# Paired last experts, earlier transposes, and split work moved from GpSimd to VectorE in a two-block transformer kernel

## The chip, the cores and the metric

One core of a Trainium2 chip runs the whole program. TensorE multiplies matrices, VectorE and ScalarE work on tiles and read TensorE's results out of PSUM, GpSimd does some work on tiles too, SyncE issues the loads of weights. Each engine runs its own queue in program order and waits on semaphores for the others. The metric is the time of one launch in device microseconds (us), lower is better.

## The reference, cut to what matters

256 tokens of width 1024 go through two blocks. The first block (an SGU with differential attention, memory attention, then a layer of 32 experts, two per token) is followed by a norm and by the second block: a layer with a convolution and a layer with causal attention, each between two SwiGLU FFNs of inner width 2816.

```python
def swiglu(x, w_gate, w_up, w_down):
    return (jax.nn.silu(x @ w_gate) * (x @ w_up)) @ w_down
...
def expert_rows(args):
    xb, e = args
    g = xb @ w_gate[e]
    u = xb @ w_up[e]
    return (jax.nn.silu(g) * u) @ w_down[e]
...
# layer 1 of the second block: 12 heads of 64, one block of keys, causal
s_own = jnp.einsum('bhqd,bhjd->bhqj', q_c, k_own).astype(jnp.float32) * scale
s_own = jnp.where(k_pos[None, :] <= q_pos[:, None], s_own, -jnp.inf)
...
h = h + jnp.concatenate([primary, mem_out], axis=-1) @ w_o[layer]
h = h + 0.5 * swiglu(rms_norm_2(h, ffn2_norm_g[layer]), ...)
```

## The kernel before, in words

**Products in three passes.** In the second block an fp32 product is made of three fp32r ones: hi by hi, lo by hi, hi by lo. `split` makes hi (a copy on ScalarE, L174) and lo (raw minus hi, L175) of each tile of weights, 2048 columns in four pieces of 512 or in two of 1024. lo runs on VectorE unless a caller gives `lo_engine`; `values` and the attention's output projection give GpSimd. `xT` transposes the tokens X and `hilo` splits them: on ScalarE (L201) and VectorE (L202) for the inputs, which the traces call x, x.

**The experts.** `Moe.run` takes the experts in eight groups of E = 4, each with C = 32 slots, so that four experts share one 128-row tile. `weights` streams gate, up and down (two raw tiles of 1 MB per expert and matrix; the last group's in halves of 512 KB), `some` multiplies: gate, up, `hidden` (silu by up), `hidden_T` (four transposes, L866, and a copy, L868), down. All four experts of a group go through each of these steps together.

**The FFNs.** `Ffn.run` works on 11 chunks of 256 inner columns; a chunk's weights are two `half` tiles (h0, h1) of 512 input rows each. `ahead` splits chunk 0's two halves early. The first chunk is multiplied as the tokens are transposed: the tokens come in pieces of two (`xT(..., range(2))`, then `range(2, 4)` as `more`). The second chunk uses `ws[0]` and `ws[1]`; then `turned` transposes g, the hidden of chunk 0 (L1053), splits it into hh and hl, and `down` multiplies it by w_down into acc.

**The causal attention.** `Second.attention` makes queries (`heads`: norm, rope, transposes at L1463), then values in three steps (`values`), with `head_pair` steps between: scores, two mask products per head (a 128x128 mask times the identity, for the diagonal blocks of the two token tiles), softmax (maximum L340, exponential L345, reciprocal L346, scaling L1238), transposes, product with the values. Then `out_proj` multiplies by w_o in four chunks c0 to c3.

**What sets the order.** The code's generators are stepped by hand (`step`, `drain`), and the tile framework's scheduler orders each engine's queue by that and by what is ready; `issue_after(ins)` keeps an instruction behind ins in that order. The second block has three raw buffers and three of hi and of lo; a load waits for the splits that read its buffer.

Of the kernel before, what the change touches and what calls it, by code (L numbers as in the profile page):

```python
# [10 lines left out]
F32 = mybir.dt.float32  # L11
# [6 lines left out]
P = 128  # L18
# [653 lines left out]
class Moe:  # L672
# [180 lines left out]
    def hidden(self, w2, gb, ub):  # L853

        k, nc = self.k, self.k.nc
        h = w2.tile([P, 512], F32, tag="mh", name=k.name("mh"), bufs=1)
        nc.scalar.activation(h, gb, AF.Silu)
        nc.vector.tensor_tensor(out=h, in0=h, in1=ub, op=ALU.mult)  # L858
        return h

    def hidden_T(self, w2, h, tag="mm"):
        k, nc = self.k, self.k.nc
        hb = k.bank(tag)
        h = h.rearrange("s (p i) -> s i p", i=4)
        for f in range(4):
            nc.tensor.transpose(hb[:, f * P : (f + 1) * P], h[:, f, :], k.ident)  # L866
        hT = w2.tile([P, 4, P], F32, tag="mhT", name=k.name("mhT"), bufs=1)
        nc.scalar.activation(hT, hb.rearrange("p (f s) -> p f s", f=4), AF.Copy)  # L868
        return hT
# [25 lines left out]
    def weights(self):  # L895


        k, a = self.k, self.k.a
        for e in range(0, 32, E):
            for nm, i in (("w_gate", 8), ("w_up", 8), ("w_down", 4)):  # L900
                for half in range(2):
                    w = [k.raw() for _ in range(E)]
                    n = 2 if e >= 32 - E else 1
                    for c in range(n):
                        c = slice(2048 * c // n, 2048 * (c + 1) // n)
                        for j in range(E):
                            src = a[nm][0, e + j].rearrange("(p i) n -> p (i n)", i=i)[:, 2048 * half : 2048 * half + 2048]
                            k.nc.sync.dma_start(w[j][:, c], src[:, c])
                    yield [v.rearrange("p (a b) -> p a b", a=i // 2) for v in w]

    def some(self, w2, xg, side, pending, ws):

        k = self.k
        slots = [slice(j * C, (j + 1) * C) for j in range(E)]
        banks = []
        for _ in range(2):
            b = k.bank()
            for half in range(2):
                w = next(ws)
                for i in range(4):  # L920
                    kk = 4 * half + i
                    for j, s in enumerate(slots):
                        k.mm(b[s, :], xg[half][:, i, s], w[j][:, i, :], kk == 0, kk == 7)
# [769 lines left out]
```

## Time and profile before

| what | value |
|---|---|
| median of 3 runs | 1687.4 us (1686.13 to 1688.68) |
| profiled execution's own time | 1684.22 us |
| its span | 1682.6 us, mean granted clock 0.984 |
| TensorE busy | 1564.2 us, 93% |
| VectorE, ScalarE, GpSimd busy | 790.7 us, 676.0 us, 102.5 us |
| loads from HBM | 406.70 MB |

The span runs from the first to the last instruction; the execution's own time is 1.6 us more, and the median is 3.2 us above that. The stages, as the timeline has them: first block without experts to about 260 us, experts to about 701, FFN to 890, convolution layer to 995, two FFNs to 1390 (the keys among them), causal attention to 1495, last FFN to the end.

### The profile page before, as it was taken

The page shows a single profiled execution, that of the slowest core. Times are in us where ns is not written, and L with a number is a line of the kernel's source. Part 1 is how long each engine was busy: PE and PEld are TensorE (multiplying, and loading weights), DVE is VectorE, ACT ScalarE, POOL GpSimd, SP SyncE. Part 2 cuts the span into 40 slices and gives each one's busy share as a digit, 9 for nine tenths or more (in the row PEclk, how much of TensorE's full clock was granted, in tenths as well). Part 3 has the DMA queues.
Part 4 walks back from the last instruction along what each step waited for, and adds up shares of the span by engine and source line. Part 5 has one row for each costly group of instructions (what it writes and reads, how often), then busy time and mean ns, then how long its engine had stood idle before and what let it go on. Part 6 is the DMA issues. An engine that isn't in the chain of part 4 may idle for free.

```text
span 1682.6 us, 21321 instructions
## 1 busy us (share of the span) xinstructions
PE 1564.2 (93%) x8326; PEld 1118.4 (66%) x8326; DVE 790.7 (47%) x1478; ACT 676.0 (40%) x1265; POOL 102.5 (6%) x122
## 2 busy tenths in 40 slices
PE   8999998868868878899999999999999999999999
PEld 7888873312212222388889878888788887688887
DVE  5875661101011101365556875555665456655544
ACT  7556641000000000254446464444654446654442
POOL 3100000000000000002000010000010004410000
PEclk9999999999999999999999999999999999999999
DMA  8638479999999999955655636565555553345552
GB/s 281 200 131 298 162 273 390 420 421 421 420 421 421 421 420 410 368 164 176 218 185 178 190 104 198 176 200 176 174 196 180 182 193 126 101 150 186 190 187 88
DMA packets 182997, 412.10 MB, mean 245 GB/s; under 512 B 10618, under 2 KB 127564, under 8 KB 161388
## 3 DMA queue, kind: packets, MB, share of 16 engines
q1 hardware_dynamic: 180630, 409.81, 67.7%
q8 instruction: 67, 1.10, 0.3%
q10 hardware_dynamic: 2086, 0.72, 0.2%
q14 instruction: 38, 0.31, 0.1%
q0 software_dynamic: 176, 0.17, 0.0%
HBM read 406.70 MB, written 1.05 MB: 242 GB/s over the span
## 4 chain that ended last, share of the span: by engine, by line
PE 55%; DMA 25%; DVE 2%; ACT 1%; issue 1%; POOL 0%; SPq 0%; ACTq 0%; POOLq 0%; DVEq 0%
PE mm L80 35%; PE acc L80 18%; DMA raw<-in_w_down_dram 8%; DMA raw<-in_w_up_dram 8%; DMA raw<-in_w_gate_dram 8%; PE mm L1053 1%; PE mm L213 1%; DVE lo L175 1%; DMA raw<-in_ffn_w_up_dram 1%; ACT hi L174 0%; PE mm L1223 0%; DVE ne L1238 0%; POOL hst L90 0%; SPq L1016 0%; DVE rope L1443 0%
## 5 line engine op out<-in xcount | busy, mean ns | idle before, releaser
L175 DVE TENSOR_TENSOR lo<-raw,hi 128x512 fp32r<-128x512 f32 (+1 forms) x596 | 468.1, 828 | 294.4 <-ACT hi L174 293.2
L80 PE MATMUL mm<-hi,x 128*128 128x512 f32 (+1 forms) x1728 | 549.3, 391 | 4.6 <-DVE x L202 3.6
L174 ACT ACTIVATE hi<-raw 128x512 fp32r<-128x512 f32 (+1 forms) x620 | 415.2, 724 | 339.0 <-PE mm L80 141.4
L80 PEld LDWEIGHTS mm<-hi,x 128*128 128x128 f32 x1728 | 324.4, 189 | 70.0 <-DVE x L202 4.1
L80 PE MATMUL mm<-lo,x 128*128 128x512 f32 (+1 forms) x864 | 334.7, 387 | 1.7 <-DVE lo L175 1.7
L80 PE MATMUL mm<-raw,xg 128*32 128x512 f32 x1024 | 200.8, 676 | 75.6 <-DMA raw<-in_w_up_dram 43.6
L80 PEld LDWEIGHTS mm<-raw,xg 128*32 128x32 f32 x1024 | 42.8, 121 | 224.0 <-DMA raw<-in_w_up_dram 87.9
L80 PEld LDWEIGHTS mm<-lo,x 128*128 128x128 f32 x864 | 163.6, 189 | 33.2 <-DVE lo L175 2.4
L80 PE MATMUL acc<-hi,hh 128*128 128x512 f32 x352 | 138.1, 392 | 0.0
L80 PE MATMUL acc<-lo,hh 128*128 128x512 f32 x352 | 137.1, 389 | 0.0
L80 PE MATMUL acc<-hi,hl 128*128 128x512 f32 x352 | 136.6, 390 | 0.0
L858 DVE TENSOR_TENSOR mh<-mh,mm 128x512 f32<-128x512 f32 x8 | 5.5, 687 | 257.7 <-PE mm L80 257.7
L80 PE MATMUL mm<-x,hi 128*128 128x256 f32 x640 | 118.7, 286 | 2.1 <-DVE x L202 1.1
L80 PE MATMUL acc<-hi,x 128*128 128x512 f32 (+1 forms) x352 | 110.2, 386 | 2.0 <-ACT x L198 2.0
L80 PE MATMUL acc<-raw,mhT 128*32 128x512 f32 x512 | 104.6, 598 | 5.9 <-DMA raw<-in_w_down_dram 5.0
L80 PEld LDWEIGHTS mm<-x,hi 128*128 128x128 f32 x640 | 100.0, 191 | 4.3 <-DVE x L202 1.8
L80 PE MATMUL mm<-x,lo 128*128 128x256 f32 x320 | 90.5, 283 | 0.0
L1043 ACT ACTIVATE g<-mm,rs 128x256 f32<-128x256 f32 x88 | 41.5, 475 | 112.0 <-PE mm L80 110.6
L80 PEld LDWEIGHTS acc<-hi,x 128*128 128x128 f32 x352 | 65.2, 188 | 15.9 <-ACT x L198 2.9
L80 PEld LDWEIGHTS acc<-hi,hh 128*128 128x128 f32 x352 | 66.1, 188 | 14.5 <-ACT hh L198 1.5
L80 PEld LDWEIGHTS acc<-hi,hl 128*128 128x128 f32 x352 | 66.1, 188 | 14.4 <-DVE hl L199 0.5
L80 PEld LDWEIGHTS acc<-lo,hh 128*128 128x128 f32 x352 | 66.1, 188 | 13.4
(346 smaller groups left out, 1326.0 us busy)
## 6 DMA issues: line engine op xcount, KB each, us to landing
raw<-in_w_gate_dram SPq DMA_DIRECT2D x56, 1024.0 KB
raw<-in_w_up_dram SPq DMA_DIRECT2D x56, 1024.0 KB
raw<-in_w_down_dram SPq DMA_DIRECT2D x56, 1024.0 KB
raw<-in_ffn_w_gate_dram SPq DMA_DIRECT2D x88, 512.0 KB
raw<-in_ffn_w_up_dram SPq DMA_DIRECT2D x88, 512.0 KB
raw<-in_ffn_w_down_dram SPq DMA_DIRECT2D x44, 1024.0 KB
raw<-in_w_in_dram SPq DMA_DIRECT2D x9, 1024.0 KB
raw<-in_w_kv_mem_dram SPq DMA_DIRECT2D x8, 1024.0 KB
```

The source lines that it names most:

```text
L80: return self.nc.tensor.matmul(out, l, r, start=start, stop=stop, skip_group_check=True).ins
L174: nc.scalar.activation(hi[:, c], v[:, c], AF.Copy)
L175: ins = lo_engine.tensor_tensor(out=lo[:, c], in0=v[:, c], in1=hi.bitcast(F32)[:, c], op=ALU.subtract).ins
L213: nc.tensor.transpose(b[:, kk * S + t * P : kk * S + (t + 1) * P], X[:, t, k * P : (k + 1) * P], self.ident)
L858: nc.vector.tensor_tensor(out=h, in0=h, in1=ub, op=ALU.mult)
L1043: nc.scalar.activation(g, b[:, :S], AF.Silu, scale=rs[:, t : t + 1])
L1053: nc.tensor.transpose(b[:, j * S + t * P : j * S + (t + 1) * P], gs[t][:, j * P : (j + 1) * P], k.ident)
```

## The change

Six edits. (1) In the last group of experts (28 to 31) gate is loaded and multiplied for all four, up, hidden, transposes and down in two pairs. (2) Before the first FFN of the second block, the split of chunk 0's second half comes behind the first pieces of x, with both loads issued as before. (3) In every FFN the last k of four of `ws[1]` is multiplied after `turned`. (4) The second part of the values' weights and w_o of the attention get their lo on VectorE. (5) A head's two mask products become one, with a mask kept twice. (6) The first step of the output projection, its splits too, is ordered behind the copy of the values.

```diff
-    def hidden(self, w2, gb, ub):
+    def hidden(self, w2, gb, ub, h=None, r=slice(0, P)):
...
+        gb, ub = k.bank(), k.bank()
+        wide(gb, range(E))
+        h, hTs = None, []
+        for n, js in enumerate(parts):
+            r = slice(js[0] * C, (js[-1] + 1) * C)
+            wide(ub, js)
+            h = self.hidden(w2, gb, ub, h, r)
+            if n == len(parts) - 1 and pending is not None:
+                pending()
+            hTs.append(self.hidden_T(w2, h, "mm", r, ("mhT", "oh")[n]))
...
+                    each = [(hf, v, j) for hf in range(2) for v, j in zip(w, js)]
+                    if last and f == 3:
+                        each.sort(key=lambda t: t[2])
...
     def ahead(self):
-        self.pre = [self.half(0, h, 4) for h in range(2)]
+        for _ in self.ahead_by_half():
+            pass
+
+    def ahead_by_half(self):
+        v = [self.loaded(0, h) for h in range(2)]
+        self.pre = []
+        for h in range(2):
+            self.pre.append(self.k.split(v[h], pieces=4))
+            yield
...
         gs = hidden(b0)
-        k.proj_tok(b1, ws[1], x, 4, 4, False, True)
+        k.proj_tok(b1, tuple(v[:, :3] for v in ws[1]), x, 4, 3, False, False)
         h = turned(gs)
+        k.proj_tok(b1, tuple(v[:, 3:] for v in ws[1]), x, 7, 1, False, True)
...
-            k.proj_tok(banks, k.wrows(a["w_kv_2"], 512 * kk, 1024, 512, nc.gpsimd), x, 4 * kk, 4, kk == 0, kk == 1)
+            k.proj_tok(banks, k.wrows(a["w_kv_2"], 512 * kk, 1024, 512), x, 4 * kk, 4, kk == 0, kk == 1)
...
-            nc.scalar.activation(self.v[:, t, 256:], banks[t][0], AF.Copy, scale=rs[:, t : t + 1])
+            self.v_ins = nc.scalar.activation(self.v[:, t, 256:], banks[t][0], AF.Copy, scale=rs[:, t : t + 1]).ins
...
-            k.mm(sc[j][:, :P], self.identr, self.maskr, False, True)
-            k.mm(sc[j][:, 2 * P : 3 * P], self.identr, self.maskr, False, True)
+            k.mm(sc[j].rearrange("p (a b) -> p a b", a=2)[:, :, :P], self.identr, self.maskr, False, True)
...
-        out = k.out_proj(w_o, cat, ahead=ahead, lo_engine=nc.gpsimd)
-        step(out, att, out, att)
+        out = k.out_proj(w_o, cat, ahead=ahead)
+        with k.tc.issue_after(self.v_ins):
+            step(out)
+        step(att, out, att)
...
-                F[1, 0].ahead()
+                pre = F[1, 0].ahead_by_half()
+                step(pre)
...
                 k.xT(X, [(x, fg)], range(2))
+                with tc.issue_after(k.behind[1]):
+                    step(pre)
```

VectorE's queue where the first FFN of the second block begins: lo are the low parts of the weights (first h0, then h1, then chunk 1), x the low parts of the tokens. Before:

```order
L175 TENSOR_TENSOR lo_4761<-raw_4757,hi_4760 128x512 x4
L175 TENSOR_TENSOR lo_4774<-raw_4770,hi_4773 128x512 x4
L202 SCALAR_TENSOR_TENSOR x_4756<-mm_4793,fg,x_4755 128x256
L202 SCALAR_TENSOR_TENSOR x_4756<-mm_4802,fg,x_4755 128x256
L1249 TENSOR_REDUCE cmask<-ident 128x32
L202 SCALAR_TENSOR_TENSOR x_4756<-mm_4793,fg,x_4755 128x256
L202 SCALAR_TENSOR_TENSOR x_4756<-mm_4802,fg,x_4755 128x256
L1275 MEMSET ch 128x6x2
```

After:

```order
L175 TENSOR_TENSOR lo_4773<-raw_4766,hi_4772 128x512 x4
L202 SCALAR_TENSOR_TENSOR x_4765<-mm_4792,fg,x_4764 128x256
L202 SCALAR_TENSOR_TENSOR x_4765<-mm_4801,fg,x_4764 128x256
L1282 TENSOR_REDUCE cmask<-ident 128x32
L1308 MEMSET ch 128x6x2
L202 SCALAR_TENSOR_TENSOR x_4765<-mm_4792,fg,x_4764 128x256
L202 SCALAR_TENSOR_TENSOR x_4765<-mm_4801,fg,x_4764 128x256
L175 TENSOR_TENSOR lo_4811<-raw_4769,hi_4810 128x512 x4
```

The first two x, in the order before behind eight lo, stand behind four, and h1's four lo behind all four x of the first pieces.

TensorE's queue in the same FFN, at the end of the second chunk (mm<-hi,x and mm<-lo,x its products, mm<-ident,g the transposes of chunk 0's hidden, acc the down product). Before:

```order
L80 MATMUL mm_4892<-hi_4909,x_4755 128x512
L80 MATMUL mm_4892<-lo_4910,x_4755 128x512
L80 MATMUL mm_4892<-hi_4909,x_4756 128x512
L1053 MATMUL mm_4996<-ident,g_4966 128x128 x2
L1053 MATMUL mm_4996<-ident,g_4969 128x128 x2
L80 MATMUL mm_5047<-hi_5052,x_4755 128x512
L80 MATMUL mm_5047<-lo_5053,x_4755 128x512
L80 MATMUL mm_5047<-hi_5052,x_4756 128x512
L80 MATMUL mm_5047<-hi_5052,x_4755 128x512
L80 MATMUL acc_4819<-hi_5013,hh_5001 128x512
```

After:

```order
L80 MATMUL mm_4901<-lo_4919,x_4764 128x512
L80 MATMUL mm_4901<-hi_4918,x_4765 128x512
L1085 MATMUL mm_4999<-ident,g_4975 128x128 x2
L1085 MATMUL mm_4999<-ident,g_4978 128x128 x2
L80 MATMUL mm_4900<-hi_4918,x_4764 128x512
L80 MATMUL mm_4900<-lo_4919,x_4764 128x512
L80 MATMUL mm_4900<-hi_4918,x_4765 128x512
L80 MATMUL mm_4901<-hi_4918,x_4764 128x512
L80 MATMUL mm_4901<-lo_4919,x_4764 128x512
L80 MATMUL mm_4901<-hi_4918,x_4765 128x512
L80 MATMUL acc_4828<-hi_5022,hh_5004 128x512
```

The transposes stand six products earlier, ahead of the last k, and acc's first product directly behind that k.

VectorE's queue in the softmaxes of the causal attention, at the third pair of heads (smx the maxima and reciprocals, ne the scaled weights, x a split of the attention's output). Before:

```order
L340 TENSOR_REDUCE smx_10931<-acc_10921 128x1
L346 RECIPROCAL smx_10931<-smx_10931 128x1
L340 TENSOR_REDUCE smx_10937<-acc_10921 128x1
L1238 TENSOR_SCALAR ne_10933<-ne_10933,smx_10931 128x128
L340 TENSOR_REDUCE smx_10943<-acc_10922 128x1
L199 TENSOR_TENSOR x_10672<-mm_10955,x_10671 128x256
L346 RECIPROCAL smx_10937<-smx_10937 128x1
L1238 TENSOR_SCALAR ne_10939<-ne_10939,smx_10937 128x256
L346 RECIPROCAL smx_10943<-smx_10943 128x1
L340 TENSOR_REDUCE smx_10949<-acc_10922 128x1
L1238 TENSOR_SCALAR ne_10945<-ne_10945,smx_10943 128x128
```

After:

```order
L340 TENSOR_REDUCE smx_10935<-acc_10927 128x1
L175 TENSOR_TENSOR lo_11245<-raw_11242,hi_11244 128x512
L346 RECIPROCAL smx_10935<-smx_10935 128x1
L340 TENSOR_REDUCE smx_10941<-acc_10927 128x1
L1271 TENSOR_SCALAR ne_10937<-ne_10937,smx_10935 128x128
L340 TENSOR_REDUCE smx_10947<-acc_10928 128x1
L199 TENSOR_TENSOR x_10682<-mm_10959,x_10681 128x256
L175 TENSOR_TENSOR lo_11245<-raw_11242,hi_11244 128x512
L346 RECIPROCAL smx_10941<-smx_10941 128x1
L346 RECIPROCAL smx_10947<-smx_10947 128x1
L340 TENSOR_REDUCE smx_10953<-acc_10928 128x1
L1271 TENSOR_SCALAR ne_10943<-ne_10943,smx_10941 128x256
```

Two of the four lo of w_o's first chunk, which stood in GpSimd's queue, stand here between the steps of the softmaxes; the other two follow, and c1 and c2 are spread over the next pairs in the same way, twelve in all.

## Rows read from the trace of the kernel before

**Rows 1.** Page, part 1: busy us, share of the span, instructions.

```profile
PE 1564.2 (93%) x8326; PEld 1118.4 (66%) x8326; DVE 790.7 (47%) x1478; ACT 676.0 (40%) x1265; POOL 102.5 (6%) x122
```

**Rows 2.** Chain that ended last, 640 to 720 us: start, length, what.

```profile
705.68 4.82 DVE lo L175 x8
710.50 0.41 DVE x L202
...
710.95 3.78 PE mm L80 x8
714.74 1.46 PE mm L213 x8
```

**Rows 3.** Timeline of TensorE, 672 to 712 us: start, length, [idle before].

```profile
682.15 0.75 PE L866 MATMUL mm<-ident,mh 128*128 128x128 f32 x4 [0.85 <-DVE mh L858]
683.64 18.15 PE L80 MATMUL acc<-raw,mhT 128*32 128x512 f32 x64 [0.75 <-ACT mhT L868]
...
710.95 1.65 PE L80 MATMUL mm<-hi,x 128*128 128x512 f32 x3 [3.65 <-DVE x L202]
```

**Rows 4.** Timeline of TensorE's weight loads, 683 to 702 us.

```profile
699.89 0.14 PEld L80 LDWEIGHTS acc<-raw,mhT 128*32 128x32 f32 x2 [0.30 <-DMA raw<-in_w_down_dram]
```

**Rows 5.** Windows: length, busy (instructions) by engine, granted clock, DMA.

```profile
704.00:708.00 4.00, 2.87 (x14) 1.54 (x12) 4.00 (x7) 4.00 (x9) 0.00 (x0) 1.00 0.69 195
710.00:712.00 2.00, 1.05 (x3) 0.85 (x4) 2.00 (x6) 1.01 (x3) 0.00 (x0) 0.50 1.08 353
716.00:718.00 2.00, 2.00 (x11) 1.64 (x10) 1.79 (x4) 1.35 (x4) 0.00 (x0) 1.00 0.19 70
```

**Rows 6.** Chain that ended last, 720 to 760 us.

```profile
719.88 15.42 PE mm L80 x68
735.31 0.44 PE mm L1053 x4
...
736.67 5.65 PE acc L80 x24
...
752.75 5.44 PE acc L80 x24
```

**Rows 7.** Timeline of ScalarE, 724 to 733 us.

```profile
729.87 0.84 ACT L1043 ACTIVATE g<-mm,rs 128x256 f32<-128x256 f32 x2 [0.75 <-DVE rs L1591]
```

**Rows 8.** Timeline of VectorE, 1409 to 1422 us.

```profile
1411.00 1.77 DVE L1125 TENSOR_TENSOR bk<-bk,hst 128x512 f32<-128x512 f32 x1 [1.25 <-POOL hst L90]
1412.69 1.77 DVE L175 TENSOR_TENSOR lo<-raw,hi 128x512 fp32r<-128x512 f32 x1
1414.39 2.62 DVE L1443 TENSOR_TENSOR rope<-bk,rope_tab 128x128 f32<-128x128 f32 x2
```

**Rows 9.** Timeline of GpSimd, 1406 to 1470 us.

```profile
1410.93 5.93 POOL L175 TENSOR_TENSOR lo<-raw,hi 128x512 fp32r<-128x512 f32 x4
```

**Rows 10.** Chain that ended last, 1380 to 1500 us.

```profile
1407.11 0.69 DVE bk L1125
...
1418.66 7.24 PE mm L80 x48
1425.90 1.45 PE acc L80 x12
```

**Rows 11.** Timeline of TensorE, 1415 to 1420 us.

```profile
1418.03 0.63 PE L1463 MATMUL mm<-ident,bk 128*128 128x128 f32 x4 [3.32 <-DVE bk L1445]
```

**Rows 12.** Windows in the attention, columns as in group 5.

```profile
1420.00:1422.00 2.00, 2.00 (x12) 2.00 (x11) 1.58 (x7) 1.67 (x4) 0.17 (x1) 0.50 0.85 332
1440.00:1470.00 30.00, 26.75 (x182) 17.19 (x181) 22.45 (x84) 23.22 (x79) 7.36 (x6) 1.00 0.29 94
1444.00:1448.00 4.00, 2.42 (x20) 1.59 (x20) 3.50 (x10) 3.13 (x12) 3.37 (x3) 1.00 0.76 251
```

**Rows 13.** Timeline of VectorE, 1438 to 1456 us.

```profile
1444.87 1.37 DVE L1238 TENSOR_SCALAR ne<-ne,smx 128x128 f32<-128x128 f32 x1
...
1450.10 0.27 DVE L1238 TENSOR_SCALAR ne<-ne,smx 128x128 f32<-128x128 f32 x1
```

More of the change, by code (lines that the diff above doesn't have):

```diff
@@ L898, in weights, with parts, some, wide @@
         k, a = self.k, self.k.a
+        every = range(E)
         for e in range(0, 32, E):
+            last = e + E == 32
+            parts = self.parts(last)
+            n = 2 if last else 1
             for nm, i in (("w_gate", 8), ("w_up", 8), ("w_down", 4)):
[L901 to L911, printed above, removed]
+                for js in (every,) if nm == "w_gate" else parts:
+                    for half in range(2):
+                        w = [k.raw() for _ in js]
+                        for c in range(n):
+                            c = slice(2048 * c // n, 2048 * (c + 1) // n)
+                            for v, j in zip(w, js):
+                                src = a[nm][0, e + j].rearrange("(p i) n -> p (i n)", i=i)[:, 2048 * half : 2048 * half + 2048]
+                                k.nc.sync.dma_start(v[:, c], src[:, c])
+                        yield [v.rearrange("p (a b) -> p a b", a=i // 2) for v in w]
+    def parts(self, last):
+        return (range(E // 2), range(E // 2, E)) if last else (range(E),)
+    def some(self, w2, xg, side, pending, ws, last):
         k = self.k
+        parts = self.parts(last)
         slots = [slice(j * C, (j + 1) * C) for j in range(E)]
-        banks = []
-        for _ in range(2):
-            b = k.bank()
+        def wide(b, js):
             for half in range(2):
@@ L921, in some @@
                     kk = 4 * half + i
-                    for j, s in enumerate(slots):
-                        k.mm(b[s, :], xg[half][:, i, s], w[j][:, i, :], kk == 0, kk == 7)
-            banks.append(b)
-        h = self.hidden(w2, *banks)
-        if pending is not None:
-            pending()
-        hT = self.hidden_T(w2, h)
-        y = [k.bank("acc") for _ in range(2)]
-        for half in range(2):
-            w = next(ws)
-            for i in range(2):
-                f = 2 * half + i
-                for hf in range(2):
-                    for j, s in enumerate(slots):
-                        k.mm(y[hf][s, :], hT[:, f, s], w[j][:, i, hf * 512 : hf * 512 + 512], f == 0, f == 3)
+                    for v, j in zip(w, js):
+                        k.mm(b[slots[j], :], xg[half][:, i, slots[j]], v[:, i, :], kk == 0, kk == 7)
+        gb, ub = k.bank(), k.bank()
[8 more added lines that the diff above has]
+            hTs.append(self.hidden_T(w2, h, "mm", r, ("mhT", "oh")[n]))
+        y = [k.bank("acc") for _ in range(2)]
+        for n, js in enumerate(parts):
+            for half in range(2):
+                w = next(ws)
+                for i in range(2):
+                    f = 2 * half + i
+                    each = [(hf, v, j) for hf in range(2) for v, j in zip(w, js)]
+                    if last and f == 3:
+                        each.sort(key=lambda t: t[2])
+                    for hf, v, j in each:
+                        l = hTs[n][:, f, slots[j - js[0]]]
+                        k.mm(y[hf][slots[j], :], l, v[:, i, hf * 512 : hf * 512 + 512], f == 0, f == 3)
         return self.combine(w2, y, *side)
@@ L994, in run @@
                 side = self.scatter_side(w2, oh, self.W[:, :, e : e + E])
-                pending = self.some(w2, xg, side, pending, weights)
+                pending = self.some(w2, xg, side, pending, weights, e + E == 32)
                 with tc.issue_after(ready):
@@ L1010, in half, with loaded @@
     def half(self, c, h, pieces=2):
+        return self.k.split(self.loaded(c, h), pieces=pieces)
+    def loaded(self, c, h):
         k = self.k
```

23 lines of the change are left out of this document (13 added, 10 removed).

## Prediction

> **What bounds the kernel now.** I read the busy shares first: TensorE has 1564.2 of 1682.6 us [rows 1]. Every other engine is at half of that or below, so a saving counts only where TensorE, or the loads during the experts, stand still for it. The chain that ended last then shows where TensorE stood still at the places that the change touches, the timelines say for what, and windows show the granted clock there. Three places matter.
>
> At the first FFN of the second block the chain goes through eight lo on VectorE (705.68, 4.82 us), one x, and then eight products [rows 2]. TensorE waited 3.65 us for that x [rows 3]. The granted clock was 1.00 (2.4 GHz) from 704 to 708, while TensorE was busy for 2.87 of 4 us; it fell to 0.50 (1.2 GHz) during this wait and was 1.00 again from 716 [rows 5]. So the eight products took 3.78 and the eight transposes behind them 1.46 us.
>
> In the attention TensorE waited 3.32 us for a bk, a key or query after rope [rows 11]. Ahead of that stand a bk and a lo of 1.77 us each and two rope operations of 2.62 [rows 8], where another bk of the same shape took 0.69 [rows 10]. At that time GpSimd ran four lo, 5.93 us from 1410.93 on [rows 9]. After the wait the granted clock was 0.50 once more from 1420 to 1422 [rows 12], and 48 products took 7.24 us [rows 10].
>
> From 1440 to 1470, in the softmaxes, no engine is full: TensorE 26.75, VectorE 22.45, ScalarE 23.22 of 30 us [rows 12]. They take turns, so here the length hangs on VectorE and ScalarE.
>
> **The change part by part.** All terms are against the profiled execution, 1684.22 us.
>
> *Experts in pairs.* The last group's loads keep their sizes and their number, and the last load is followed by the same four passes. What a pair can save is TensorE's wait for hidden, 0.85 and 0.75 us [rows 3]. But TensorE is still waiting for a load of w_down at 699.89 [rows 4], after the 64 down passes began at 683.64: both waits are made up long before the end, and the loads set it. Silu, product and copy run twice on half the partitions; the first pair's lie under the second pair's loads, and the second pair's cost what the four's did. I take 0. If the waits were not covered, it could give up to 1.6 back or cost as much again; I keep -0.3 to +0.3, since only the order of the last passes differs.
>
> *The first FFN's split behind x.* Four lo of the eight go behind the x: four of 4.82/8 = 0.60 us, 2.4 us. TensorE would resume at 708.5, after 1.2 us of waiting instead of 3.65. With so short a wait I take the clock to stay at 1.00. At that level a product takes 15.42/68 = 0.227 us [rows 6], eight 1.81, and eight transposes 2 x 0.44 = 0.88 [rows 6]. Instead of 3.78 + 1.46 = 5.24 us that is 2.69: another 2.5 us. The four lo that now come later follow the four x and end at about 712.7. TensorE has the eight products, the eight transposes (to 711.2) and twelve more products of h0, 2.7 us, ahead of the first one of h1, at 713.9: covered by 1.2 us, and each lo of h1 serves a later product than the one ahead of it. Without the cover TensorE would wait up to 1 us. Later loads that wait for h1's buffer go out 2.2 us later and are not next. Together -4.9, bounds -2.4 (the clock falls all the same) and -5.2.
>
> *Transposes earlier.* Directly after the transposes of g, the 24 products of acc take 5.65 us, elsewhere 5.44 [rows 6]; they wait for hh and hl. Six products more between, 1.4 us, cover that. It happens in four FFNs: 4 x 0.21 = -0.8. The opposite danger is that g is late. The first two g start at 729.87 on ScalarE [rows 7], the transposes at 735.31 [rows 6]. The transposes come 1.4 us earlier, and in this first FFN all of TensorE's queue another 4.9, so here they stand at about 729. The g wait for a norm factor [rows 7], which comes from X by way of ScalarE and VectorE; I take it to be 2 to 3 us earlier, since both stood waiting for x before, and g then to be ready at about 728.6. If it were not earlier, TensorE would wait some 2 us there. I take -0.8, bounds +1.0 and -1.0.
>
> *GpSimd's lo to VectorE, up to the values.* Without the four lo beside them, bk goes back from 1.77 to 0.69 us, lo from 1.77 to 0.60, and the two rope operations, at the same ratio, from 2.62 to about 1.0: 3.8 us, more than the wait of 3.32, so the wait goes: -3.3. With no wait the clock should stay up; 48 products of 256 columns at half of 0.227 are 5.5 us instead of 7.24: -1.7. VectorE gets eight lo of the values, 4.8 us, of which the 3.8 us freed pay most.
>
> *One mask per head.* 12 score and mask products take 1.45 us [rows 10], 0.12 each, which is what a product of 256 columns takes too (5.5/48 = 0.115). So two for four saves 0.24 a pair of heads. For the first two pairs this is on TensorE's path: -0.5. The other four lie in the softmax section, where TensorE has room: 0. The Trainium skill, in "TensorE: Matmul & The Clock Gate", section "Back-to-back issue gap", speaks against this term: the time between two products grows with the columns, so one of 256 costs as much as two of 128. By that rule the term would be nearly 0 and the time 1679.2; the row shows 0.12 for a product of 128 columns, so the trace does not agree, and I go by the row.
>
> *w_o's lo in the softmaxes.* TensorE reaches the end of the values 3.3 + 1.7 + 0.5 = 5.5 us earlier. But from there VectorE has twelve more lo of 0.60, 7.2 us, and the copies to hi on ScalarE, eight of them formerly earlier, fall into the same section. Against that, a softmax operation beside GpSimd took 1.37 us and the same shape 0.27 without [rows 13]; some 2 us of such slowing go. VectorE's 7.5 us of idle time in the 30 are gaps between turns, and a lo of 0.6 fits some of them. Of 5 us net I take half as hidden: +2.5. Bounds: 0 (all in the gaps) and +7.2 (none, and the four lo of c3 as well, less the 2). The rest of the projection is bound by TensorE as before.
>
> Attention together: -5.5 + 2.5 = -3.0. Sum: 0 - 4.9 - 0.8 - 3.0 = -8.7, and 1684.2 becomes 1675.5. The median of the runs is 3.2 us above the profiled execution, so in the terms of the median: 1687.4 - 8.7 = 1678.7.
>
> **The rivals.**
>
> *The softmaxes fill up.* VectorE's turns are all on the chain, and each lo delays the next softmax: +7.2 instead of +2.5, the sum is -4.0, 1683.4. For it: 22.45 + 7.2 is 29.65 of 30. Against it: the lo are spread singly, and VectorE's gaps are there. If the first FFN's clock does not hold either, the sum is -1.5 and the time 1685.9, no change that a measurement can tell (about 0.2%, 3.4 us). Chance 0.2 for the first, 0.08 for both.
>
> *The clock at the first FFN falls all the same.* TensorE still has short waits around 704 to 708; if they suffice, only 2.4 us are gained there, and the time is 1681.2. For it: the clock fell within 3.65 us of waiting and stayed low till 716. Against it: from 1444 to 1448 TensorE was busy for only 2.42 of 4 us at a clock of 1.00 [rows 12]. Chance 0.15.
>
> *The clock falls in the softmaxes (the other side).* Longer turns leave TensorE more often without work. If a wait there comes to the 3.3 us that went ahead of the drop at 1420, the rest of the section runs at 1.2 GHz: of the 26.75 us of work say half, 13 us, doubles: -8.7 + 13 = +4.3, 1691.7. It decides from waits of that length; the window with least work before kept its clock. Chance 0.05.
>
> *The pairs cost.* The last passes of the pairs queue behind each other and the loads no longer cover them: up to +1.6, within the range. And *the order does nothing*: the lo that go to VectorE could be late for the values; then a wait of the old length stands at the values and the attention gives about 0: 1681.7, chance 0.05.
>
> **How the numbers follow.** My forecast, 1676 to 1681 with its likeliest value at 1678.7, gets 0.45 with the small terms' bounds; the rivals 0.2, 0.08, 0.15, 0.05 and 0.05, and 0.02 is left for what I do not see. The lowest bounds together, -0.3 - 5.2 - 1.0 - 5.5, give 1675.4; the runs spread by 1.3 us to each side, half of which I add: 1674.8. The upper end takes in the softmaxes filled, and nearly all of that with the clock fallen: 1685.5. Faster by over 0.2% is below 1684.0: the forecast, the fallen clock, late values and 0.14 of the first rival, 0.79; slower is the clock in the softmaxes and a little of what I do not see, 0.06; the rest, 0.15, is within 0.2%.
>
> **What would show it.** In the profile after: TensorE's wait at the first FFN near 1.2 us and windows from 708 to 716 at 1.00; acc's 24 products at 5.44 in four FFNs; no GpSimd lo, bk 0.69 and rope near 1.0 for two at the values and no wait of 3.3; TensorE at the end of the values 5.5 us nearer to the start of the attention; the softmax section 2 to 3 us longer, with VectorE near 27 of 30 busy. The experts end at the same time. It would be wrong if the section of the softmaxes grew by 7 us or more, if the clock fell in it, or if h1's split held up TensorE at the first FFN.

## The result, and the profile after

| | kernel before | changed kernel |
|---|---|---|
| median | 1687.4 us (1686.13 to 1690.01, 5 runs) | 1677.96 us (1677.44 to 1679.85, 5 runs) |
| ratio | | 0.9949, 95% interval 0.9938 to 0.9961 |
| profiled execution, span | 1684.22 us, 1682.6 us | 1679.85 us, 1678.2 us |

The change takes 0.5%, some 8.6 us by the ratio; the forecast was 1678.7 in a range of 1674.8 to 1685.5. The two profiled executions differ by only 4.4 us: the one before is 3.2 us below its median, the one after 1.9 above. So I compare by stages. The table gives the length from one stage's first transposes of the tokens to the next stage's, in us, and below it the difference (the first FFN of the kernel before ends at 899.5; the 890 in the list of stages ahead of the prediction is too early).

| | start to first FFN | first FFN | convolution layer | second FFN | third FFN and keys | attention | last FFN |
|---|---|---|---|---|---|---|---|
| before | 704.16 | 195.34 | 95.70 | 187.08 | 206.41 | 101.28 | 192.60 |
| after | 705.24 | 190.49 | 100.08 | 186.80 | 206.14 | 97.21 | 192.27 |
| difference | +1.08 | -4.85 | +4.38 | -0.28 | -0.27 | -4.07 | -0.33 |

The five stages in which the change was to gain give -9.8. The two others, the first (the experts in pairs, costed at 0) and the convolution layer (not costed), give +5.5 in this pair of executions; how much of that belongs to the change is a question for the experiments.

Page, part 1, of the kernel after (as [rows 1]): GpSimd has lost 32 us, VectorE has not gained as much.

```profile
PE 1566.6 (93%) x8318; PEld 1121.9 (67%) x8318; DVE 795.6 (47%) x1503; ACT 676.3 (40%) x1268; POOL 70.4 (4%) x98
```

TensorE's timeline at the first FFN (as [rows 3]), and the windows there (as [rows 5]; length, busy by engine, granted clock behind the five pairs).

```profile
709.63 1.00 PE L80 MATMUL mm<-hi,x 128*128 128x512 f32 x3 [1.24 <-DVE x L202]
```

```profile
708.00:710.00 2.00, 0.76 (x4) 0.30 (x2) 2.00 (x5) 1.00 (x3) 0.00 (x0) 1.00 0.83 260
710.00:712.00 2.00, 2.00 (x12) 1.57 (x11) 2.00 (x6) 1.00 (x3) 0.00 (x0) 1.00 1.07 366
```

The wait for x is 1.24 us instead of 3.65, and the clock stays at 1.00 through it. In the chain behind it (as [rows 6]) the transposes of g have six products behind them, and acc's 24 take 5.46 instead of 5.65 us; no wait for g shows.

```profile
730.35 0.44 PE mm L1085 x4
730.78 1.39 PE mm L80 x6
732.17 5.46 PE acc L80 x24
```

VectorE's timeline ahead of the values (as [rows 8]) and the chain of the attention (as [rows 10]):

```profile
1411.30 0.69 DVE L1158 TENSOR_TENSOR bk<-bk,hst 128x512 f32<-128x512 f32 x1 [1.53 <-POOL hst L90]
1411.91 0.68 DVE L175 TENSOR_TENSOR lo<-raw,hi 128x512 fp32r<-128x512 f32 x1
1412.51 0.48 DVE L1476 TENSOR_TENSOR rope<-bk,rope_tab 128x128 f32<-128x128 f32 x2
...
1413.79 2.49 DVE L175 TENSOR_TENSOR lo<-raw,hi 128x512 fp32r<-128x512 f32 x4
```

```profile
1414.32 0.87 PE mm L1496 x8
1415.20 5.75 PE mm L80 x48
1420.95 1.29 PE acc L80 x10
...
1429.42 5.47 PE mm L80 x24
...
1468.99 0.87 PE mm L1256 x8
```

bk takes 0.69 and the two ropes 0.48 us; the four lo that were GpSimd's follow them. TensorE goes through without the wait of [rows 11], and its 48 products take 5.75 instead of 7.24 us. Eight score products and two masks take 1.29 where twelve took 1.45. From the stage's first transposes to the end of the values it is 46.1 us, 5.4 less than before (51.6). From there to the last heads' transposes (1468.99 here, 1473.01 before), the section of the softmaxes, it is 34.1 us against 32.7.

The convolution layer shows what nothing in the change was meant to touch: a wait for a shifted copy of the layer's input (ch, copied between partitions by DMA for the convolution's products), and a fall of the clock, which comes 13 us behind the wait, while TensorE runs 24 products of one column (acc<-ones,ch). TensorE's timeline and the windows of the kernel after:

```profile
945.01 7.55 PE L80 MATMUL mm<-ch,wst 128*32 128x256 f32 x134
953.89 7.07 PE L80 MATMUL mm<-ch,wst 128*32 128x256 f32 x122 [1.33 <-DMA ch<-ch]
...
964.79 3.57 PE L80 MATMUL acc<-ones,ch 128*128 128x1 f32 x24
```

```profile
964.00:968.00 4.00, 4.00 (x31) 3.62 (x30) 2.98 (x10) 3.59 (x13) 0.00 (x0) 0.84 0.01 2
968.00:972.00 4.00, 4.00 (x13) 3.21 (x14) 1.72 (x8) 0.00 (x0) 0.70 (x1) 0.50 0.00 0
972.00:976.00 4.00, 3.95 (x18) 2.57 (x19) 1.95 (x7) 2.25 (x6) 0.00 (x0) 0.81 0.00 0
```

The kernel before had neither: its 256 products ran through in 14.45 us and the clock was 1.00 up to the layer's end. Its timeline, and its window at the products of one column:

```profile
948.78 14.45 PE L80 MATMUL mm<-ch,wst 128*32 128x256 f32 x256
```

```profile
968.00:972.00 4.00, 4.00 (x30) 3.61 (x30) 2.92 (x13) 2.00 (x8) 0.70 (x1) 1.00 0.01 2
```

### The profile page after: what moved, and what is told of

The parts are those of the page before. It is cut to its first block, busy times and chain, and to the rows that moved or that the text cites. A ratio compares the mean times of both kernels' runs of the same rounds, so it can differ in the third digit from the quotient of the medians.

```text
span 1678.2 us, 21307 instructions
## 1 busy us (share of the span) xinstructions
PE 1566.6 (93%) x8318; PEld 1121.9 (67%) x8318; DVE 795.6 (47%) x1503; ACT 676.3 (40%) x1268; POOL 70.4 (4%) x98
## 4 chain that ended last, share of the span: by engine, by line
PE 56%; DMA 26%; ACT 1%; DVE 0%; issue 0%; SPq 0%; ACTq 0%
PE mm L80 34%; PE acc L80 20%; DMA raw<-in_w_down_dram 9%; DMA raw<-in_w_up_dram 8%; DMA raw<-in_w_gate_dram 8%; PE mm L1085 1%; PE mm L213 1%; DMA raw<-in_ffn_w_up_dram 0%; DMA ch<-ch 0%; PE mm L1256 0%; ACT ne L345 0%; ACT hi L174 0%; DVE lo L175 0%; SPq L1040 0%; ACTq L1318 0%
## 5 line engine op out<-in xcount | busy, mean ns | idle before, releaser
L175 DVE TENSOR_TENSOR lo<-raw,hi 128x512 fp32r<-128x512 f32 (+1 forms) x620 | 483.4, 822 | 291.4 <-ACT hi L174 287.1
L859 DVE TENSOR_TENSOR mh<-mh,mm 128x512 f32<-128x512 f32 (+1 forms) x9 | 6.2, 687 | 257.8 <-PE mm L80 257.8
```

The source lines that it names most:

```text
L175: ins = lo_engine.tensor_tensor(out=lo[:, c], in0=v[:, c], in1=hi.bitcast(F32)[:, c], op=ALU.subtract).ins
L859: nc.vector.tensor_tensor(out=h[r], in0=h[r], in1=ub[r], op=ALU.mult)
```

## The experiments

My theory after the first comparison: each edit works where the forecast put it, by its own wait and by the clock behind the wait, and the loss in the convolution layer is chance. Rivals: the loss there follows from the change, the attention's gain is from the masks or the order and not from GpSimd, and the experts in pairs cost what the later start shows. All times below are medians beside a run of the kernel before on the same chip. The stage lengths of all profiles, as differences to the kernel before's first profile:

| kernel | start to first FFN | first FFN | convolution | attention | median us | ratio (95%) |
|---|---|---|---|---|---|---|
| e1 first FFN alone | +0.45 | -4.40 | +2.26 | -0.04 | 1683.56 | 0.9979 (0.9970 to 0.9988) |
| e2 transposes alone | +0.92 | +0.10 | +0.34 | -1.04 | 1685.82 | 0.9997 (0.9988 to 1.0006) |
| e3 attention alone | +1.52 | +0.18 | +2.27 | -3.89 | 1683.96 | 0.9982 (0.9972 to 0.9992) |
| e4 pairs alone | +0.88 | -0.35 | +2.64 | +0.20 | 1688.90 | 1.0007 (0.9998 to 1.0016) |
| e5 values on GpSimd | +0.22 | -3.33 | +2.22 | +1.96 | 1683.63 | 0.9977 (0.9969 to 0.9986) |
| e6 w_o on GpSimd | +0.70 | -3.24 | +2.24 | -3.96 | 1681.35 | 0.9968 (0.9957 to 0.9980) |
| e7 two masks | +0.73 | -4.80 | +1.01 | +0.77 | 1683.96 | 0.9978 (0.9968 to 0.9988) |
| e8 no order behind the values | +0.69 | -3.24 | +2.28 | -0.75 | 1681.07 | 0.9963 (0.9951 to 0.9975) |
| e9 changed kernel again | +1.01 | -4.81 | +4.34 | -4.09 | 1679.70 | 0.9955 (0.9941 to 0.9968) |
| e10 changed, filled | +0.42 | -4.82 | +0.89 | -4.10 | 1676.51 | 0.9942 (0.9928 to 0.9955) |
| e11 before, filled | +0.41 | -2.20 | +0.84 | +0.22 | 1683.82 | 0.9987 (0.9977 to 0.9996) |
| e12 one mask alone | +0.77 | -0.15 | +2.23 | -0.10 | 1686.90 | 0.9998 (0.9989 to 1.0007) |

The medians of e1 to e4, e5 to e8 and e9 to e12 stand beside 1686.62, 1686.72 and 1687.18 us of the kernel before.

The kernel before's first profile, from which the differences are taken, is the shortest of all fourteen in two columns, the start and the convolution layer; a loss there is thus no sign of the change by itself. To the first FFN all others take 0.2 to 1.5 us longer, e1 to e3 too, which leave the experts as they were. In the convolution layer the loss goes with two things. The 256 products with their waits for ch took 14.45 to 15.95 us. And the clock held in five profiles (before, e2, e7, e10, e11), with a loss of 0 to 1.0 us; it fell in seven, with 2.2 to 2.6; and in after and e9, with 4.3 and 4.4, it stayed low about twice as long as in those seven.

### e1: the first FFN's edit alone

```diff
...
-                F[1, 0].ahead()
+                pre = F[1, 0].ahead_by_half()
+                step(pre)
...
+                with tc.issue_after(k.behind[1]):
+                    step(pre)
```

> The kernel before with the second edit alone (chunk 0's second half split behind the first pieces of x). My theory: 4.65 us less, as between the two traces at the first FFN, about 1682.8 where the kernel before has 1687.4; TensorE's wait there 1.2 us instead of 3.65, the clock at 1.00 throughout. Rival (given back): the profile after lost 4.4 us in the convolution layer, where TensorE waited 1.3 us for the last shifted copy and the clock fell behind it; if that follows from TensorE coming there earlier, this kernel shows the same wait and the gain is near 0.

It is 0.21% faster, 3.5 us by the ratio. The stage is 4.4 us shorter, with TensorE's wait as in the changed kernel:

```profile
709.00 1.01 PE L80 MATMUL mm<-hi,x 128*128 128x512 f32 x3 [1.23 <-DVE x L202]
```

But the convolution layer of this execution is 2.26 us longer. That is no proof of the rival: e3, e4 and e12, which reach that layer no earlier, lose 2.2 to 2.6 there too.

### e2: the transposes alone

```diff
-        k.proj_tok(b1, ws[1], x, 4, 4, False, True)
+        k.proj_tok(b1, tuple(v[:, :3] for v in ws[1]), x, 4, 3, False, False)
         h = turned(gs)
+        k.proj_tok(b1, tuple(v[:, 3:] for v in ws[1]), x, 7, 1, False, True)
```

> The kernel before with the third edit alone (transposes six products earlier in four FFNs). My theory: 0.8 to 1.0 us less, acc's 24 products at 5.45 in all four places. Rival: nothing, because the earlier transposes wait for g in the first FFN; then TensorE shows a wait of up to 2 us for g there.

The time can't tell 0.8 us (interval 0.9988 to 1.0006). The trace can: acc's 24 products behind the transposes take 5.44 us in the first FFN, the second FFN is 0.29 us shorter, the third 0.17, the last 0.29. The first FFN as a whole shows nothing (+0.10); but that stage differs by 0.35 in e4 too, where nothing in it was changed, with when its fallen clock comes back. No wait for g shows, so the rival is out. The attention, unchanged here, is 1.0 us shorter: TensorE waited 3.31 us for bk as before, but the clock did not fall behind it, and the values' 48 products took 5.74 us. It fell later, in the softmaxes of this unchanged attention, behind a wait of 1.71 us; that section is 33.26 us long, 0.5 more than in the kernel before:

```profile
1448.00:1452.00 4.00, 4.00 (x20) 2.46 (x18) 3.23 (x13) 3.24 (x13) 1.16 (x1) 0.59 0.37 106
```

### e3: the attention alone

```diff
-            k.proj_tok(banks, k.wrows(a["w_kv_2"], 512 * kk, 1024, 512, nc.gpsimd), x, 4 * kk, 4, kk == 0, kk == 1)
+            k.proj_tok(banks, k.wrows(a["w_kv_2"], 512 * kk, 1024, 512), x, 4 * kk, 4, kk == 0, kk == 1)
...
+            k.mm(sc[j].rearrange("p (a b) -> p a b", a=2)[:, :, :P], self.identr, self.maskr, False, True)
...
+        out = k.out_proj(w_o, cat, ahead=ahead)
+        with k.tc.issue_after(self.v_ins):
+            step(out)
...
```

> The kernel before with the fourth, fifth and sixth edits alone (lo on VectorE, one mask product, values copied first). My theory: 4.1 us less, all of it between TensorE's first and last product of the attention, 5.4 of it up to the end of the values, 1.3 given back in the softmaxes. Rival: the softmaxes give back less or more when they meet other loads; then the two parts differ from these by over 1 us.

As expected: the attention is 3.89 us shorter in the trace, 3.0 us by the times. Up to the end of the values it is 5.5 us less (5.4 expected), and the softmaxes give back 1.6 (1.3 expected).

### e4: the pairs alone

```diff
+    def parts(self, last):
+        return (range(E // 2), range(E // 2, E)) if last else (range(E),)
...
+        for n, js in enumerate(parts):
+            wide(ub, js)
+            h = self.hidden(w2, gb, ub, h, r)
...
+            hTs.append(self.hidden_T(w2, h, "mm", r, ("mhT", "oh")[n]))
```

> The kernel before with the first edit alone (last four experts in two pairs). My theory: no difference, within 0.5 us, since the loads end the group. Rival: the trace after reaches the first FFN 1.08 us later than before; if that is the pairs' cost, this kernel is 1 us slower, and the last down passes end about 1 us longer after the last group's first load.

No gain. The ratio's interval, 0.9998 to 1.0016, takes in nothing and a loss of 2.7 us; the trace puts no loss at the pairs. In the changed kernel the last group's first load in the chain starts at 643.43 and the last experts' output product at 702.81, 59.38 us; in the kernel before it is 642.24 and 701.72, 59.48. The 1.08 us of the later start lie ahead of the group. The chain of e4 itself holds other loads of the group; from the long load of w_down ahead of the group to the same output product it is 83.22 us there (619.39 to 702.61), 83.26 in the kernel before and 83.17 in the changed one. Chain and timeline of the changed kernel:

```profile
643.43 10.16 DMA raw<-in_w_gate_dram
```

```profile
673.02 0.69 PE L869 MATMUL mm<-ident,mh 64*128 64x64 f32 x4 [0.84 <-DVE mh L859]
...
683.26 0.69 PE L869 MATMUL mm<-ident,mh 64*128 64x64 f32 x4 [0.85 <-DVE mh L859]
...
702.81 0.73 PE L80 MATMUL acc<-yh,ohT 128*128 128x512 f32 x2
```

The waits for hidden are still there, 0.84 and 0.85 us, once for each pair; the loads hide them as they hid the old ones.

### e5: the values' lo back on GpSimd

```diff
-            k.proj_tok(banks, k.wrows(a["w_kv_2"], 512 * kk, 1024, 512), x, 4 * kk, 4, kk == 0, kk == 1)
+            k.proj_tok(banks, k.wrows(a["w_kv_2"], 512 * kk, 1024, 512, nc.gpsimd), x, 4 * kk, 4, kk == 0, kk == 1)
```

> The changed kernel, with the values' lo given back to GpSimd (w_o's stay on VectorE). My theory (GpSimd's lo slow what VectorE does on the same stretch): the second bk and rope take 1.77 and 2.6 us again, TensorE waits about 3.3 us for bk and the clock falls behind it; the way to the end of the values is 5 us longer than in the changed kernel, so about 1683 where that has 1678. Rival (the gain is from fewer masks and from the order of the copies): the changed kernel's time within 1 us.

Waits, timeline of VectorE and a window of this kernel:

```profile
PE mm L1496 <- DVE bk L1478: 3.3, 1, 3.3
```

```profile
1409.55 1.77 DVE L1158 TENSOR_TENSOR bk<-bk,hst 128x512 f32<-128x512 f32 x1 [1.25 <-POOL hst L90]
1411.25 1.78 DVE L175 TENSOR_TENSOR lo<-raw,hi 128x512 fp32r<-128x512 f32 x1
1412.95 2.62 DVE L1476 TENSOR_TENSOR rope<-bk,rope_tab 128x128 f32<-128x128 f32 x2
```

```profile
1416.00:1420.00 4.00, 3.41 (x16) 3.44 (x17) 2.71 (x12) 2.29 (x5) 1.01 (x1) 0.50 0.39 118
```

bk, the wait of 3.3 us and the half clock are all back. The attention is 6.0 us longer than the changed kernel's (5 expected). The rival is out: the gain hangs on the eight lo of the values not running on GpSimd. The first four of them, which run there beside bk, lo and rope, make the wait.

### e6: w_o's lo back on GpSimd

```diff
-        out = k.out_proj(w_o, cat, ahead=ahead)
+        out = k.out_proj(w_o, cat, ahead=ahead, lo_engine=nc.gpsimd)
```

> The changed kernel, with w_o's lo given back to GpSimd (the values' stay on VectorE). My theory: the gain up to the end of the values stays, and in the softmaxes twelve lo less on VectorE (7.2 us) stand against softmax operations slowed by GpSimd: within 1 us of the changed kernel, either way. Rival (VectorE's lo are what stretches the softmaxes): 2.5 us faster than the changed kernel. Second rival (GpSimd's lo now all fall into the softmaxes and slow them): over 2 us slower.

The attention takes 97.32 us, the changed kernel's 97.21, and its section of the softmaxes 34.25 us, against 34.10. So with the rest of the change in place the 16 lo of w_o cost the same on either engine; both rivals are out, and the section is 1.4 us longer than before without the move as well. VectorE's timeline in this kernel shows the price on GpSimd's side, a softmax operation (ne, 128x256) at 0.81 us, which takes 0.35 in the changed kernel:

```profile
1448.32 0.81 DVE L1271 TENSOR_SCALAR ne<-ne,smx 128x256 f32<-128x256 f32 x1
```

The first FFN, the same as the changed kernel's, is 1.6 us longer here. Its wait is the same 1.24 us, but the clock fell behind it:

```profile
709.25 1.30 PE L80 MATMUL mm<-hi,x 128*128 128x512 f32 x3 [1.24 <-DVE x L202]
```

```profile
710.00:712.00 2.00, 2.00 (x6) 1.59 (x6) 2.00 (x5) 0.61 (x2) 0.00 (x0) 0.50 1.09 370
712.00:714.00 2.00, 2.00 (x12) 1.69 (x11) 1.09 (x3) 0.52 (x2) 0.00 (x0) 0.70 1.09 347
```

### e7: two masks a head

```diff
-            k.mm(sc[j].rearrange("p (a b) -> p a b", a=2)[:, :, :P], self.identr, self.maskr, False, True)
+            k.mm(sc[j][:, :P], self.identr, self.maskr, False, True)
+            k.mm(sc[j][:, 2 * P : 3 * P], self.identr, self.maskr, False, True)
...
```

> The changed kernel with two mask products a head as before. My theory: 0.2 us longer at each of the first two pairs, 0.4 to 0.5 in all, the softmaxes unchanged; too little for the times, to be read between the transposes of the queries and the end of the values. Rival (a product costs by its columns alone): the 12 score and mask products take the same as the 10 of the changed kernel, 1.29 us.

My price was right and the expectation wrong. Twelve products take 1.45 us again, 0.16 more than ten; but the attention is 4.84 us longer than the changed kernel's. In the softmaxes the clock fell, which it did not do there in either profile of the changed kernel. The chain, at the first wait of the section, and the windows:

```profile
1417.30 1.45 PE acc L80 x12
```

```profile
1452.00:1456.00 4.00, 3.57 (x15) 1.94 (x15) 2.92 (x13) 2.24 (x9) 0.00 (x0) 0.64 0.05 7
1456.00:1460.00 4.00, 4.00 (x12) 2.19 (x11) 1.95 (x8) 1.79 (x6) 0.00 (x0) 0.50 0.80 256
```

This is the prediction's rival on the other side, in a neighbour of the changed kernel, though not by its condition, a wait of 3.3 us: the longest wait of TensorE in the section is 0.99 us, in place of 0.55. With the masks, the scheduler also put the lo and the softmax steps in another order. But the clock fell in this section of e2 too, where the attention is as before, and it held in the kernel before behind a wait of 1.58 us there. So whether the masks' products, the other order or chance did it here, this run does not tell.

### e8: the projection not ordered behind the values

```diff
...
-        with k.tc.issue_after(self.v_ins):
-            step(out)
-        step(att, out, att)
+        step(out, att, out, att)
```

> The changed kernel without the sixth edit (the projection's first step not ordered behind the copy of the values). My theory: the splits of w_o's first chunks go back ahead of the values' copies, on ScalarE and with it on VectorE, where the first pairs' softmaxes then wait: up to 2 us slower in the softmaxes, or no difference. Rival: faster by 1 us or more, since fewer lo are left for the softmaxes.

More than expected: the attention loses 3.3 us against the changed kernel. TensorE waits for the copy of the values (bv), which stands on ScalarE behind splits of w_o and softmax steps, and in this wait the clock falls:

```profile
PE mm L1239 <- ACT bv L1528: 2.4, 1, 2.4
```

```profile
1432.00:1436.00 4.00, 2.64 (x15) 2.03 (x13) 3.40 (x10) 3.39 (x9) 0.00 (x0) 1.00 0.43 177
1436.00:1440.00 4.00, 2.97 (x13) 1.99 (x14) 2.35 (x9) 4.00 (x12) 0.00 (x0) 0.60 0.51 137
```

So most of the attention's gain, 3.3 of 4.1 us in this execution, hangs on the sixth edit too; how much of the 3.3 is the wait and how much the clock, the run does not part.

### e9: the changed kernel again

> The changed kernel once more, as the measure for the runs beside it. Its first profile lost 4.4 us in the convolution layer against the kernel before, and the kernels before it with and without the second edit lost 0 to 4.4 us there. My theory (chance of the execution: the granted clock of the convolution layer falls or not): the time is 8 to 10 us below the kernel before again, and the layer's loss is another one than 4.4. Rival (the change itself costs 4.4 us there): 4 to 5 us lost again in that layer.

The time repeats (ratio 0.9955). My theory of chance does not stand as I put it: the convolution layer lost 4.34 us again, with the same wait of 1.3 us for the copies. The rival isn't shown either, since e10, which is the same program with four products more, lost 0.89; there the wait for the copies was 1.00 us and the clock held. The changed kernel's ten times lie in two heaps, 1677.2 to 1678.0 and 1679.7 to 1680.5, five in each; both profiles are of the upper one.

### e10 and e11: the waits at the first FFN filled

The same edit, with 4 products in the changed kernel and 12 in the kernel before; their result is read by nothing.

```diff
...
+            if kk == 0 and fill:
+                b = k.bank()
+                for _ in range(fill):
+                    k.mm(b, x[0][:, 0, :P], wh[:, 0, :], True, True)
             k.proj_tok(b0, (wh[:, i : i + 1], wl[:, i : i + 1]), ...)
...
```

> The changed kernel with four products of 512 columns, whose result nothing reads, ahead of the first product of the first FFN, where TensorE waits 1.24 us for x. In three of six profiles with the second edit the clock fell to 0.50 behind this wait, at a cost of 1.6 us, in three it did not. My theory (a fuller array there keeps the clock): the wait is 0.3 us, the clock stays at 1.00 from 704 to 718, the first FFN takes 190.5 to 191, and the median is up to 0.8 us below the changed kernel's. Rival (the products only delay the work): 0.9 us slower at that place.

> The kernel before with twelve products of 512 columns, whose result nothing reads, at the same place; its order and its wait for x are untouched, only the wait is filled. It takes the second edit's two terms apart. My theory (the wait itself 2.4 us, the clock behind it 2.5): TensorE goes on at the same time as before, but at 1.00, and the first FFN is 2.5 us shorter (192.8). Rival (the clock falls for another reason than the wait): 195.3 as before.

TensorE's timeline and windows, first of the kernel before, filled, then of the changed kernel, filled:

```profile
706.08 3.25 PE L80 MATMUL mm<-hi,x 128*128 128x512 f32 x13 [0.24 <-ACT x L201]
...
711.37 1.00 PE L80 MATMUL mm<-hi,x 128*128 128x512 f32 x3 [1.37 <-DVE x L202]
```

```profile
710.00:712.00 2.00, 0.63 (x4) 0.42 (x4) 2.00 (x6) 0.65 (x2) 0.00 (x0) 1.00 1.08 365
712.00:714.00 2.00, 2.00 (x13) 1.69 (x13) 1.70 (x5) 1.78 (x4) 0.00 (x0) 1.00 1.11 358
```

```profile
708.97 1.00 PE L80 MATMUL mm<-hi,x 128*128 128x512 f32 x3 [0.77 <-DVE x L202]
```

In e11 TensorE goes on 6.80 us after the stage's first transposes, before 6.79: the wait for x ends when it did. But the clock stays at 1.00, where it fell in all five profiles with this wait unfilled (before, e2, e3, e4, e12), and the stage is 2.20 us shorter. That is the clock's term by itself, forecast at 2.5. The ratio, 0.9987, agrees with 2.2 us. In e10 the wait is 0.77 (0.3 expected), the clock holds, as it did in four of the seven profiles without the filling, and the kernel is the fastest of all, 3.2 us below the changed kernel beside it; 0.8 had been expected. In the profile the rest is the convolution layer, which kept its clock in this execution. The intervals of e9 and e10 overlap, so the size of the gap is open; three of e10's five times (1675.13, 1675.60 and 1676.51) are below the lowest of e9 (1677.16).

### e12: one mask alone

> The kernel before with the fifth edit alone (one mask product a head). The changed kernel with two masks lost 4.8 us in the attention against the changed kernel, since the clock fell in the softmaxes there. My theory (a mask is worth 0.2 us a pair, and the fall came from the other order of the queues with VectorE's lo between): 0.4 to 0.6 us less in the attention here, no fall of the clock in the softmaxes. Rival (the masks themselves load TensorE so that the clock falls): 4 us less in the attention.

No gain, by the times and by the trace, but the parts of that nothing are large. TensorE's timeline, a window and the chain of this kernel:

```profile
1421.09 0.63 PE L1463 MATMUL mm<-ident,bk 128*128 128x128 f32 x4 [3.56 <-DVE bk L1445]
```

```profile
1422.00:1424.00 2.00, 2.00 (x19) 2.00 (x18) 0.78 (x4) 2.00 (x5) 1.01 (x1) 1.00 0.54 147
```

```profile
1421.72 5.74 PE mm L80 x48
...
1435.93 5.47 PE mm L80 x24
...
1475.76 0.88 PE mm L1223 x8
```

The wait for bk is there, 3.56 us, 0.24 more than in the kernel before, but the clock stayed at 1.00: the values' products take 5.74 instead of 7.24 us, -1.5 by chance. The masks of the first two pairs give -0.3. And the section of the softmaxes, from 1441.40 to 1475.76, is 34.4 us instead of 32.7, +1.6. With the longer wait that is +0.05 together, measured -0.10.

The same section, from the end of the values to the last heads' transposes, in us, in all profiles where the clock held in it (it fell there in e2, e7 and e8):

| | softmaxes |
|---|---|
| two masks, as before: before, e1, e4, e11 | 32.71 to 32.74 |
| one mask, w_o's lo on VectorE: after, e9, e10, e3, e5 | 34.10 to 34.30 |
| one mask, w_o's lo on GpSimd: e6, e12 | 34.25, 34.36 |

So the section grows by 1.4 us or more with the one mask, on either engine and in either order of the projection, and whether the clock ahead of it fell (e5) or held. The traces show where. TensorE alone over the section (length, busy, granted clock) in the kernel before, in the changed kernel and in e12:

```profile
1440.28:1473.01 32.73, 29.48 (x194) 1.00 0.26 83
```

```profile
1434.89:1468.99 34.10, 32.40 (x186) 1.00 0.30 94
```

```profile
1441.40:1475.76 34.36, 32.79 (x186) 1.00 0.28 93
```

With eight products fewer TensorE is busy 3 us longer and waits less. Of the busy time the score products, the same 48 records in all three, take 6.9 us before, 9.6 in the changed kernel and 10.4 in e12. In the kernel before, the eight score records of a pair of heads stand together in the queue; in e12 and the changed kernel those of the later pairs are parted by transposes, and one head's four alone then take as long as a pair's eight. The kernel before, then e12:

```profile
1453.48 0.93 PE L80 MATMUL acc<-bkT,bqT 64*128 64x128 f32 x8
```

```profile
1455.81 0.92 PE L80 MATMUL acc<-bkT,bqT 64*128 64x128 f32 x4
```

So the mask saves products and the scheduler's order of the others costs more than they saved. That it is this order was not tried by itself, and the mask is not the only edit that brings it: in e7, with two masks, the last pair's heads stand apart too.

## Why the prediction was right

**Experts in pairs: 0, measured -0.1.** Right, and for the reason given: the waits for hidden are still there and are made up.

**The first FFN: -4.9, measured -4.4 (e1) and, with the earlier transposes, -4.8 to -4.85 where the clock held.** The wait fell by 2.41 us as costed (2.4). The clock held, and its term alone is 2.2 (e11), costed at 2.5. The rival of a clock that falls all the same came true in e5, e6 and e8, three of the seven profiles with this edit and no filling: then the stage gains 3.2 to 3.3 us, transposes included. I had given it 0.15; it deserved nearer 0.4.

**Transposes earlier: -0.8, measured -0.28, -0.27 and -0.33 in three FFNs and 0.2 in acc of the first.** Right, a little undersized (-1.1 in all); g was not late, as the norm factor came earlier: the first two g start at 726.51 and the transposes at 730.18.

**GpSimd's lo to VectorE: -3.3 and -1.7, measured -3.3 and -1.5.** Right, and e5 shows the cause. The second term depends on the execution: behind that wait the clock fell in before, e1, e4, e5 and e11, and held in e2 and e12.

**One mask: -0.5, measured -0.3 ahead of the softmaxes and about +1.6 in them.** The step that failed is "the other four lie in the softmax section, where TensorE has room: 0": with the one mask that section is longer in every profile where its clock held, with nothing else changed too (e12), since the scores of two heads no longer stand together. Of the size, 0.16 a pair instead of 0.24: the row the argument rested on mixes masks with scores, which take less when two heads' stand together. From their start to the next product's, four masks took 0.50 us before and two 0.34 after, so a product of 256 columns costs more than one of 128, but less than two.

The rule that the prediction took from the Trainium skill, "TensorE: Matmul & The Clock Gate", section "Back-to-back issue gap", gave nearly 0. The section gives that rule for a product by itself; for a stream of weight loads and products it says that the rule counts too little at few columns (81 ns measured at 128, where the rule gives about 56), which the prediction passed over. The trace agrees with the second part: the four masks of 128 columns took 0.125 us each.

**w_o's lo in the softmaxes: +2.5, measured -0.1.** e6 against the changed kernel. The section is 1.4 us longer than before, near the size that I gave, but for another cause, the parted scores: the forecast's sum came out near partly because two errors met, and that is luck. What the lo cost on VectorE they cost on GpSimd as well, by slowing the softmax operations. The term's upper bound was also summed too low: 16 lo of 0.60, less the 2, are 7.6 and not 7.2.

**The clock in the softmaxes: a chance of 0.05, at 13 us.** It did not fall there in the changed kernel. Where it did, in e2 and e7, it fell behind waits of 1.71 and 0.99 us and not of 3.3, and the section was 0.5 and some 4.4 us longer.

The sum of these, -9.8 by the stages, is 1.1 us beyond the forecast -8.7, and the times gave -8.6 and -7.6. The difference is the convolution layer, which the prediction passed over. Its length varies from 95.7 to 100.1 us over fourteen profiles with the same instructions in it, by late copies and by the clock, and the kernel before's first profile is the shortest. That the medians of the kernel before contain some 2.2 us there fits the 3.2 us by which they exceed that profile, but it was only argued. What decides whether the clock falls there, and whether the changed kernel's earlier arrival makes the 4.4 of both its profiles more likely, is open.

## What to carry to other kernels

A wait on TensorE has two prices, its length and the clock behind it; cost both, and try whether filling the wait gives back the second. Before work is moved off an engine, look at what it slows by running: here four subtractions on GpSimd cost a wait of 3.3 us through VectorE, and 2.1 more in the products behind, where the clock fell. Fewer products are no gain where a scheduler makes another order of the rest and parts products that ran side by side: compare the stage with the edit alone, part by part, since a sum near zero can hide a clock that held by chance.

## What the runs showed of the hardware that was not expected

The same wait of 1.24 us at the same place was followed by a clock of 1.00 in some executions (after, e1, e7, e9) and of 0.50 in others (e5, e6, e8), with 1.6 us between them. So it was with the wait of 3.3 to 3.6 us at the values: a fall in before, e1, e4, e5 and e11, none in e2 and e12. A fall also came without a long wait: in e7 TensorE's longest wait in the softmaxes was 0.99 us, while the kernel before kept its clock there behind one of 1.58. In the convolution layer TensorE had been busy for 12 us ahead of the fall in after, the last part of it with 24 products of one column; in e12, where the clock fell to 0.57 in the window from 972 to 976, the profile shows no wait ahead of it in that layer's products, and the same products of one column ran at 1.00 in before and e10. So the length of the last wait alone does not tell whether the clock falls.

Score products on 64 of the 128 rows took half the time when two heads' stood together: eight records in 0.93 us, and four by themselves in 0.92.
